# A two-block transformer on one core: the mixing stage of block 2 in a new order

## The chip, the cores and the metric

The kernel runs on 1 core of one Trainium2 chip. The metric is device time in microseconds, the median over several executions. The engines are TensorE (PE, with its weight loads as PEld), VectorE (DVE), ScalarE (ACT) and GpSimd (POOL); SyncE (SP) and ScalarE's queue issue transfers.

## The reference

A sequence of 512 positions of width 1024 passes through two blocks in float32. Block 1 mixes three branches (a short convolution, block-sparse attention with relative bias, attention to a memory), merges them through gates, multiplies by `w_out` and runs a convolutional feed-forward layer (`w_up`, `w_down`). Block 2, whose mixing is what changes:

```python
h = rmsnorm_2(x, norm_mix)
hq, hf, hi, hg, sq, sk, sv, iq, ik, iw, mq = split_in(h @ w_in)
o_hg = hgrn2_mix(hq, hf, hi, hg, ...)       # 4 heads, gated recurrence, rmsnorm per head, times silu(hg)
o_sa = dsa_mix(sq, sk, sv, iq, ik, iw, ...) # 8 index heads score keys; 128 kept per query; 4 attention heads
o_mem = mem_mix(mq, rmsnorm_2(mem, norm_mem), w_mem_kv, ...)  # 4 heads over 256 memory rows
x = x + concat(o_hg, o_sa, o_mem) @ w_out
a, b = split(rmsnorm_2(x, norm_ffn) @ w_ffn_in)
x = x + (silu(a) * b) @ w_ffn_out
```

## The kernel before

Every matrix product of weights is done in three passes with a high and a low part of both operands (lines 175 to 177): hi*hi, hi*lo, lo*hi. A weight tile is 128 x 1024 floats (512 KB). `load` (line 185) brings it into one of 3 raw buffers by SP's queue; `split` (line 190) makes its high part by a cast on ScalarE (line 197) and its low part by a subtraction (line 198), on VectorE or, while `on_pool` is set, on GpSimd. One tile is 24 matmuls, mostly of 512 columns.

The order of all instructions is written out once by the class `Program`; each engine runs its own in that order. A job takes its weight tiles and issues its matmuls in parts; after each part, and after each job, `tick` lets every background generator advance by its rate: 0.5 is one step at every second tick. `start` begins a generator, `drain` steps all of them until the named one has ended, `ctl` places a function between jobs. Before each job, `run` issues the splits of tiles up to two ahead (six for the resident tiles of an output product's second half), and the raw loads up to three beyond.

- `head_chunks` runs the first chunks of a stage in two halves of 256 positions, so that the first half can start while the last positions are still normalized and transposed (`late`). `chunk` gives features on partitions, `gemm_N` gives positions on partitions. `gemm_out` is an output product of two 512-column halves; `need` names the generators that are drained before a tile of its first half.
- HGRN (`hgrn_levels`): for each of 4 heads, 10 levels. A level is subtracted on GpSimd (lines 1254 to 1261), exponentiated on ScalarE (1266 to 1271), scaled on VectorE (1274) and multiplied on TensorE (1283 to 1308), each a step later than the one before; the small levels are merged by a masked copy (1314). `gates(j)` prepares the pair of heads j from `w_hf` and `w_hq`. `hgrn_tail` makes the outputs per 128 positions for all four heads, with norm and gate, and transposes them.
- The index (`idx`): scores of 8 heads (lines 990 to 995), then 16 rounds of maximum and replacement for each of three query blocks (`top_keys`, lines 1007 and 1008), on VectorE.
- Attention (`sa_pair`, `causal_pair`): scores, softmax (592, 601), transposes, product (618). Memory attention (`mem2_pair`, `mem_heads`) is alike; its keys and values come from `memT2.build` (norm and transposes of mem_2) and `w_mkv2`.

The order in `mixing` before: head with `w_hf` and `w_hq` of the first pair; `w_ikw`; four `w_iq`; four `w_mqsv`; drain of `memT2`; four half tiles of `w_mkv2`; four `w_sqk`; `w_hf` and `w_hq` of the second pair; four `w_hi`; four `w_hg`; drain of `hgrn`; then `w_out_2`, which needs `mem2`, `sa0` and `sa1`, and `tail`, in this order.

## Time and profile before

| | |
|---|---|
| median of 3 runs | 1565.33 us (1564.37 to 1567.9) |
| the profiled execution | 1568.02 us, its span 1566.2 us |
| mean granted clock of TensorE | 0.986 of full speed |
| TensorE busy | 1520.0 us (97%) |
| VectorE, ScalarE, GpSimd busy | 789.3, 597.5, 238.3 us |

A matmul's busy time is modelled and overlaps the next one's. The granted clock has two levels, 1.00 (2.4 GHz) and 0.50 (1.2 GHz); a figure between them is a mean over a stretch. Busy time of VectorE counts overlapping instructions once in a table by stage, and each in full in a table by line.

### The profile page before, as it was taken

Reading aid. Unit: us, or ns where it says so; the run is one execution under the profiler, and the core shown is the slowest. Engines: PE = TensorE matmul, PEld = TensorE weight load, DVE = VectorE, ACT = ScalarE, POOL = GpSimd, SP = SyncE. Lnnn points to the kernel's source line nnn. Section 1 sums busy time; section 2 is a strip of 40 time slices with the busy share of each in tenths; the row PEclk is TensorE's granted clock in tenths of the full one; section 3 lists DMA queues with packets and bytes.
Section 4 is the critical chain, followed back from the end, with each engine's and each line's share of the span. In section 5 each row is a group of like instructions: output and inputs, shape, how many; then the busy total and the mean of one; then the engine's idle time right before and its main releaser. Section 6 shows DMA issues by size and latency. Waiting matters only on the chain.

```text
span 1566.2 us, 20399 instructions
## 1 busy us (share of the span) xinstructions
PE 1520.0 (97%) x8107; PEld 1261.1 (81%) x8107; DVE 789.3 (50%) x1200; ACT 597.5 (38%) x1043; POOL 238.3 (15%) x344
## 2 busy tenths in 40 slices
PE   8999999999999999999999999999789999999999
PEld 7887888888888888888888977677568888888887
DVE  5455453544446666665235488988545233333231
ACT  5454452433343433333234465455533222222120
POOL 1000000021102000000002197716220000000000
PEclk9999999999999999999999999999699999999999
DMA  5432243322252122223232331122222122222231
GB/s 187 99 106 73 83 128 108 121 81 81 96 164 78 68 95 99 102 96 107 95 137 92 115 119 70 68 75 82 68 81 81 68 94 95 94 102 100 94 121 54
DMA packets 46053, 151.83 MB, mean 97 GB/s; under 512 B 5476, under 2 KB 5988, under 8 KB 45958
## 3 DMA queue, kind: packets, MB, share of 16 engines
q1 hardware_dynamic: 41472, 142.62, 26.6%
q10 hardware_dynamic: 4486, 7.90, 1.8%
q8 instruction: 64, 1.05, 0.3%
q14 instruction: 31, 0.25, 0.0%
HBM read 145.66 MB, written 4.85 MB: 96 GB/s over the span
## 4 chain that ended last, share of the span: by engine, by line
PE 82%; DVE 7%; ACT 4%; POOL 2%; issue 2%; DMA 2%; ACTq 0%; SPq 0%; DVEq 0%; POOLq 0%
PE p L175 26%; PE p L176 26%; PE p L177 26%; PE p L307 2%; ACT s L592 1%; DVE s L1008 1%; DVE s L1274 1%; DVE m L1007 1%; PE p L618 1%; ACT s L601 1%; POOL m L228 1%; DVE wl L198 1%; DMA s<-mem 0%; POOL s L183 0%; DVE s L180 0%
## 5 line engine op out<-in xcount | busy, mean ns | idle before, releaser
L175 PE MATMUL p<-s,wh 128*128 128x512 f32 (+1 forms) x1192 | 463.6, 389 | 0.9 <-DVE t L1314 0.6
L176 PE MATMUL p<-s,wh 128*128 128x512 f32 (+1 forms) x1192 | 461.0, 387 | 0.0
L177 PE MATMUL p<-s,wl 128*128 128x512 f32 (+1 forms) x1192 | 460.7, 387 | 0.0
L198 DVE TENSOR_TENSOR wl<-r,wh 128x1024 fp32r<-128x1024 f32 x217 | 258.3, 1192 | 329.8 <-ACT wh L197 329.0
L197 ACT CAST wh<-r 128x1024 fp32r<-128x1024 f32 x233 | 232.9, 1002 | 230.8 <-PE p L176 219.2
L175 PEld LDWEIGHTS p<-s,wh 128*128 128x128 f32 x1192 | 224.0, 188 | 46.3 <-DVE t L1314 0.8
L177 PEld LDWEIGHTS p<-s,wl 128*128 128x128 f32 x1192 | 223.9, 188 | 45.5
L176 PEld LDWEIGHTS p<-s,wh 128*128 128x128 f32 x1192 | 224.0, 188 | 43.9
L175 PE MATMUL p<-wh,s 128*128 128x512 f32 x544 | 218.6, 402 | 4.1 <-ACT s L270 4.1
L177 PE MATMUL p<-wh,s 128*128 128x512 f32 x544 | 215.2, 396 | 1.0 <-DVE s L275 0.5
L176 PE MATMUL p<-wl,s 128*128 128x512 f32 x544 | 214.8, 395 | 0.0
L176 PE MATMUL p<-s,s 128*128 128x256 f32 (+1 forms) x408 | 132.2, 324 | 5.6 <-DVE s L180 5.6
L175 PE MATMUL p<-s,s 128*128 128x256 f32 (+1 forms) x408 | 133.2, 326 | 0.9 <-ACT s L268 0.8
L177 PE MATMUL p<-s,s 128*128 128x256 f32 (+1 forms) x408 | 131.6, 322 | 0.0
L183 POOL TENSOR_SCALAR s<-t 128x512 fp32r<-128x512 f32 (+1 forms) x64 | 34.7, 543 | 618.3 <-DVE t L1506 227.4
L175 PEld LDWEIGHTS p<-wh,s 128*128 128x128 f32 x544 | 104.0, 191 | 26.3 <-ACT s L270 4.5
L177 PEld LDWEIGHTS p<-wh,s 128*128 128x128 f32 x544 | 103.8, 191 | 24.2 <-DVE s L275 1.0
L176 PEld LDWEIGHTS p<-wl,s 128*128 128x128 f32 x544 | 104.1, 191 | 20.5
L176 PEld LDWEIGHTS p<-s,s 128*128 128x128 f32 x408 | 79.5, 195 | 11.9 <-DVE s L180 6.6
L175 PEld LDWEIGHTS p<-s,s 128*128 128x128 f32 x408 | 79.4, 195 | 7.1 <-ACT s L268 1.5
L177 PEld LDWEIGHTS p<-s,s 128*128 128x128 f32 x408 | 79.5, 195 | 5.3
L307 PE MATMUL p<-ident,s 128*128 128x128 f32 x400 | 59.7, 290 | 16.2 <-ACT s L601 4.8
(182 smaller groups left out, 1416.1 us busy)
## 6 DMA issues: line engine op xcount, KB each, us to landing
r<-w_up SPq DMA_DIRECT2D x44, 512.0 KB, 3.2
r<-w_ffn_in SPq DMA_DIRECT2D x44, 512.0 KB, 3.2
r<-w_in_gate SPq DMA_DIRECT2D x24, 512.0 KB, 3.2
r<-w_down SPq DMA_DIRECT2D x22, 512.0 KB, 3.2
r<-w_ffn_out SPq DMA_DIRECT2D x22, 512.0 KB, 3.2
r<-w_out SPq DMA_DIRECT2D x16, 512.0 KB, 3.2
r<-w_in_conv SPq DMA_DIRECT2D x12, 512.0 KB, 3.2
r<-w_in_qk SPq DMA_DIRECT2D x8, 512.0 KB, 4.6
```

Source lines behind the costliest of these rows:

```text
L175: mm(out, sh, mh, start=start, stop=False)
L176: mm(out, sh, ml, start=False, stop=False)
L177: mm(out, sl, mh, start=False, stop=stop)
L183: g_.tensor_scalar(out, x, s, 0.0, op0=ALU.mult, op1=ALU.add)
L197: a_.copy(hi[:, :n], raw)
L198: (g_ if on_pool else v_).tensor_tensor(out=lo[:, :n], in0=raw, in1=hi[:, :n].bitcast(F32), op=ALU.subtract)
L228: g_.tensor_tensor(out=rs, in0=ms, in1=negh[:, :n], op=ALU.pow)
L307: pe.transpose(ps[:m, n:n + P], s, ident)
L592: a_.activation(pv, pv, AF.Exp, scale=-1.0, bias=negm[s][:, i:i + 1], accum_out=sums[s][:, i:i + 1])
L601: a_.activation(pv, pv, AF.Copy, scale=rec[s][:, i:i + 1])
L618: mm(ps[64 * s:64 * s + 64, j * P:512], vh(s, j), p_view(PT, s, 3 - j), start=(j == 0), stop=(j == 3))
L1007: v_.max(m8, sc)
```

## The change

`split` always subtracts on VectorE; `on_pool` is gone. `memT2` is built during the last gate of block 1, and `w_mkv2` multiplied at the first boundary, between `w_out` and the up-projection's head, which then has two chunks instead of four. The finished keys and values go to DRAM and come back in the mixing by six transfers on SP. The mixing begins with the index's weights; `hgrn` steps at 0.7 and `idx` at 0.85 instead of 0.5 and 0.6; the second pair of gates comes earlier; the two attention pairs are one chain at 0.5; the HGRN tail is done per pair of heads and 256 positions, with the gate applied after the transposes; `w_hg` is last and is laid out with features on partitions.

```diff
-        (g_ if on_pool else v_).tensor_tensor(out=lo[:, :n], in0=raw, in1=hi[:, :n].bitcast(F32), op=ALU.subtract)
+        v_.tensor_tensor(out=lo[:, :n], in0=raw, in1=hi[:, :n].bitcast(F32), op=ALU.subtract)
...
     for m in range(KD):
+        if m == 3:
+            pr.start("memT2", lambda: memT2.build())
         gate(2, m, use_bc(m, True))
+    pr.drain("memT2")
...
+    def filled_head(late, srcs, uses):
+
+        def first():
+            late[0](2)
+            late[1]()
+        head_chunks(srcs, H, uses, {(0, 0): first, (0, 1): lambda: late[0](3)})
...
-    next_head((late, swap), [W[0], W[NFF], W[1], W[NFF + 1]], [use_up_a(0), use_up_g(0), use_up_a(1), use_up_g(1)])
-    for j in range(2, NFF):
+    gemm_N([io["w_mkv2"][i] for i in range(4)], lambda: memT2, lambda t, ps: use_mkv2(t, ps), nt=2)
+    filled_head((late, swap), [W[0], W[NFF]], [use_up_a(0), use_up_g(0)])
+    pr.start("kv2", lambda: fin_mkv2())
+    for j in range(1, NFF):
...
-        yield
+        yield from wait(2)
+        st["kvd"] = drp.tile([3, P, 1024], F32, name="kvd")
+        for n, x in enumerate((m2.pop("kh").all, m2.pop("kl").all, m2.pop("v"))):
+            nc.sync.dma_start(st["kvd"][n], x.rearrange("p a b -> p (a b)").bitcast(F32))
+
+    def load_kv2():
+        m2["kh"], m2["kl"], m2["v"] = Heads(256), Heads(256), slot([P, 4, 256])
+        for n, x in enumerate((m2["kh"].all, m2["kl"].all, m2["v"])):
+            nc.sync.dma_start(x.rearrange("p a b -> p (a b)").bitcast(F32), st["kvd"][n])
...
-    def use_hg(t, ps):
-        if t % 2 == 0:
-            gS[t // 2] = slot([P, 2, 512])
-        silu2(gS[t // 2][:, t % 2, :], ps)
+    def use_hg(c):
+        def f(ps):
+            if c % 2 == 0:
+                gS[c // 2] = slot([P, 2, 512])
+            silu2(gS[c // 2][:, c % 2, :], ps)
+            if c % 2:
+                hg["gate", c // 2] = True
+        return f
...
-        g_.tensor_tensor(out=y, in0=y, in1=gS[t // 2][:, t % 2, :], op=ALU.mult)
         return y
...
+    def hgrn_outT(j, tp, y):
+
+        pt = transposes([y[:, (2 * t + k) * P:(2 * t + k + 1) * P] for k in range(2) for t in range(2)])
+        cols = slice(tp * 256, tp * 256 + 256)
+        z = tmp()
+        v_.scalar_tensor_tensor(z.rearrange("p (k t) -> p k t", k=2), pt.rearrange("p (k t) -> p k t", k=2),
+                                vcol(V_HG), gS[j][:, :, cols], op0=ALU.mult, op1=ALU.mult)
+        mixed.alloc(j)
+        hi, lo = mixed.h[j][:, :, cols], mixed.l[j][:, :, cols]
+        z = z.rearrange("p (k t) -> p k t", k=2)
+        a_.copy(hi, z)
+        sub_lo(lo, z, hi)
+
+    def hgrn_tail(j):
+        def g():
+            while ("done", 2 * j + 1) not in hg:
+                yield
+            y1 = hgrn_out(j, 1)
+            yield from wait(2)
+            y0 = hgrn_out(j, 0)
+            yield from wait(2)
+            while ("gate", j) not in hg:
+                yield
+            hgrn_outT(j, 1, y1)
+            yield from wait(2)
+            hgrn_outT(j, 0, y0)
+        return g
...
     def mixing():
+        next_head((late2, swap2), M["w_ikw"] + M["w_iq"][:3], [use_ikw, use_iq(0), use_iq(1), use_iq(2)], park)
+        pr.start("idx", chain(sel0, index_weights, *(index_scores(c) for c in range(4)), top_keys(3),
+                              top_keys(2), top_keys(1)), 0.85)
+        pr.start("hgrn", hgrn_levels, 0.7)
+        chunk(M["w_iq"][3], H, use_iq(3))
+        for c in (0, 1):
+            chunk(M["w_hf"][c], H, use_hf(c))
+        for c in (0, 1):
+            chunk(M["w_hq"][c], H, use_hq(c))
         pr.start("gates0", gates(0))
+        gemm_N(M["w_mqsv"], H, use_mqsv)
+        pr.ctl(load_kv2)
+        pr.start("finm", fin_mq)
+        for c in (2, 3):
+            chunk(M["w_hf"][c], H, use_hf(c))
+        pr.drain("finm")
+        pr.start("mem2", chain(mem2_pair(0), mem2_pair(1)), 0.5)
+        for c in (2, 3):
+            chunk(M["w_hq"][c], H, use_hq(c))
+        pr.start("gates1", gates(1))
+        gemm_N(M["w_sqk"], H, use_sqk)
+        pr.start("fin", fin_sqk)
+        gemm_N(M["w_hi"], H, use_hi)
+        pr.start("tail0", hgrn_tail(0))
+        pr.start("sa", chain(sa_pair(0), sa_pair(1)), 0.5)
+        pr.start("tail1", hgrn_tail(1))
         for c in range(4):
+            chunk(M["w_hg"][c], H, use_hg(c))
...
-             need={0: ("mem2",), 1: ("sa0", "sa1"), 2: ("tail",)})
+             need={0: ("mem2",), 1: ("sa",), 2: ("tail0", "tail1")})
...
-    io["w_hg"] = _pack_n(w[:, 1536:2048])
+    io["w_hg"] = _pack_t(w[:, 1536:2048])
```

The lines of the old `mixing` that go are left out here; its order is told above.

## Rows read from the trace of the kernel before

**Rows 1.** The page: the span, the busy time of each engine with its share and number of instructions, and the granted clock in 40 equal slices, in tenths.
```profile
span 1566.2 us, 20399 instructions
...
PE 1520.0 (97%) x8107; PEld 1261.1 (81%) x8107; DVE 789.3 (50%) x1200; ACT 597.5 (38%) x1043; POOL 238.3 (15%) x344
...
PEclk9999999999999999999999999999699999999999
```

**Rows 2.** The table by stage: stretch in us, its length, then busy time and number of instructions for PE, PEld, DVE, ACT and POOL, the mean granted clock, the DMA engines' share and GB/s.
```profile
477.00:503.00 26.00, 22.99 (x150) 21.05 (x149) 17.99 (x34) 11.62 (x34) 6.29 (x13) 0.93 0.19 61
...
912.00:944.00 32.00, 26.07 (x176) 20.67 (x175) 26.63 (x29) 19.59 (x44) 25.67 (x26) 1.00 0.35 126
944.00:969.00 25.00, 25.00 (x260) 19.61 (x259) 19.64 (x39) 16.88 (x35) 19.22 (x19) 0.93 0.22 77
969.00:998.00 29.00, 28.18 (x269) 21.91 (x267) 26.48 (x52) 13.45 (x26) 23.57 (x27) 1.00 0.29 99
998.00:1034.00 36.00, 33.59 (x226) 25.40 (x227) 33.12 (x77) 17.98 (x43) 16.48 (x21) 1.00 0.16 56
1034.00:1069.00 35.00, 31.85 (x136) 23.43 (x134) 27.04 (x56) 19.62 (x39) 13.90 (x30) 0.95 0.17 57
1069.00:1098.00 29.00, 29.00 (x315) 22.83 (x317) 24.44 (x60) 16.45 (x35) 13.55 (x18) 1.00 0.26 92
1098.00:1126.00 28.00, 16.55 (x295) 14.09 (x286) 18.89 (x70) 18.09 (x49) 10.23 (x20) 0.55 0.24 77
1126.00:1150.00 24.00, 23.27 (x161) 18.80 (x160) 9.36 (x16) 6.52 (x12) 9.24 (x14) 0.95 0.07 23
1150.00:1162.00 12.00, 7.42 (x39) 5.57 (x37) 8.46 (x11) 7.54 (x12) 1.48 (x2) 1.00 0.48 168
1162.00:1171.00 9.00, 8.48 (x24) 6.37 (x25) 1.64 (x5) 0.27 (x1) 0.00 (x0) 0.62 0.35 126
```

**Rows 3.** The same table for a quiet stretch of block 2's feed-forward layer.
```profile
1240.00:1280.00 40.00, 40.00 (x178) 33.14 (x177) 12.83 (x14) 9.90 (x12) 1.86 (x3) 1.00 0.31 105
```

**Rows 4.** The chain that ended last, 921 to 945 us: start, length, what.
```profile
922.23 7.52 DMA s<-mem
```

**Rows 5.** The same chain, 1148 to 1165 us.
```profile
1154.12 3.22 DMA r<-w_out
...
1157.42 1.05 ACT s L197
```

**Rows 6.** The list of transfers: what, queue, how many, size of each, median us from issue to landing.
```profile
s<-xdram SPq DMA_DIRECT2D x4, 512.0 KB, 4.0
```

**Rows 7.** VectorE's instructions by line, 882 to 1165 us: out<-in, shapes, number, total busy us, mean ns of one, idle time before them.
```profile
L1274 DVE TENSOR_TENSOR s<-s,s 128x256 f32<-128x256 f32 x36 | 28.8, 800 | 2.7 <-ACT s L1271 2.7
L1007 DVE MAX8 m<-s 128x8 f32<-128x512 f32 (+2 forms) x48 | 26.5, 552 | 0.2
L1008 DVE MATCH_REPLACE8 s<-m,s 128x512 f32<-128x512 f32 (+2 forms) x48 | 26.0, 542 | 0.0
...
L1056 DVE SCALAR_TENSOR_TENSOR s<-p,gsc,s 64x256 fp32r<-64x256 f32 x16 | 7.7, 483 | 2.4 <-ACT s L1054 2.1
...
L1314 DVE COPY_PREDICATED t<-lmask,p 128x128 f32<-128x128 uint32 x24 | 7.1, 295 | 2.6 <-PE p L1308 1.4 <-POOL t L1312 1.2
L993 DVE TENSOR_SCALAR s<-t,iw 128x512 f32<-128x512 f32 (+2 forms) x3 | 5.6, 1855 | 1.5 <-ACT t L990 1.4
...
L633 DVE TENSOR_REDUCE m<-p 128x2 f32<-128x512 f32 x8 | 5.5, 682 | 0.0
L1065 DVE SCALAR_TENSOR_TENSOR s<-p,vecs,s 128x256 fp32r<-128x256 f32 x12 | 5.2, 477 | 0.1
...
L1033 DVE TENSOR_REDUCE m<-t 128x4 f32<-128x256 f32 (+1 forms) x10 | 5.1, 522 | 4.1 <-ACT t L1031 4.1
L1183 DVE TENSOR_TENSOR_SCAN s<-t,t 128x512 f32<-128x512 f32 x4 | 4.9, 1225 | 0.1
L198 DVE TENSOR_TENSOR s<-r,s 128x1024 fp32r<-128x1024 f32 x4 | 4.8, 1220 | 3.3 <-ACT s L197 3.3
...
L1008 DVE MATCH_VALUE_LOAD s<-m,s 128x8 f32 x48 | 4.4, 92 | 1.7
```

**Rows 8.** Line 1274 over the whole span: duration in ns, shortest, median and longest; first and last start.
```profile
L1274 DVE TENSOR_TENSOR s<-s,s x36: 411/474/2607, 917.3 to 1113.4; 128x256 f32<-128x256 f32 x36
```

**Rows 9.** TensorE in order of time, 1087 to 1088 us: start, length, line, operation, number.
```profile
1087.26 0.46 PE L1308 MATMUL p<-s 128*32 128x32 f32 x32
1087.65 0.50 PE L175 MATMUL p<-wh,s 128*128 128x512 f32 x1
```

**Rows 10.** GpSimd's instructions by line, 882 to 1165 us, columns as in rows 7.
```profile
L198 POOL TENSOR_TENSOR wl<-r,wh 128x1024 fp32r<-128x1024 f32 x16 | 39.1, 2445 | 14.6 <-ACT wh L197 11.3 <-issue 3.0 <-DVE s L1274 0.3
```

**Rows 11.** VectorE in order of time, from 923 to 930 us and from 1059 to 1061 us, columns as in rows 9.
```profile
925.01 2.61 DVE L1274 TENSOR_TENSOR s<-s,s 128x256 f32<-128x256 f32 x1
...
1059.37 1.98 DVE L198 TENSOR_TENSOR wl<-r,wh 128x1024 fp32r<-128x1024 f32 x1 [0.94 <-ACT wh L197]
```

**Rows 12.** GpSimd in order of time, from 923 to 929 us.
```profile
924.63 2.70 POOL L198 TENSOR_TENSOR wl<-r,wh 128x1024 fp32r<-128x1024 f32 x1
```

**Rows 13.** ScalarE in order of time, from 1113 to 1127 us; a row can merge many instructions of a line.
```profile
1118.16 7.33 ACT L601 ACTIVATE s<-s,m 128x512 f32<-128x512 f32 x16
```

92 lines of the change are left out of this document (28 added, 64 removed).

## The prediction, made before the changed kernel was run

> **What bounds the kernel now.** I read the page first: TensorE (PE) is busy 97% of the span [rows 1], so time can only come from stretches where it waits or runs at the lower of its two clock levels. The table by stage finds them [rows 2]. A quiet stage issues 178 matmuls of 512 columns in 40 us, 0.225 us each [rows 3]; any stage with PE under its own length, or PEclk under 1.00, loses against that. Read idle time as length minus PE, and the clock's share as (1 - PEclk) times PE's busy time (times the length where PE is nearly always busy).
>
> - 477 to 503, from `w_out` to the up-projection's head: 3.0 idle and 1.8 of clock, 4.8 us.
> - 912 to 969, the drain of `memT2`: 5.9 idle and 1.8 of clock, 7.7 us. The longest piece of its chain is the load of mem_2, 7.5 us [rows 4].
> - 969 to 1098: 0.8 + 2.4 + 3.2 idle and 1.8 of clock, 8.2 us. Here VectorE (DVE) is the neighbour at its limit: 33.1 of 36 us in one stage.
> - 1098 to 1126, the drain of `hgrn`: 11.5 idle, and 0.45 of the 16.5 busy, 7.4: 18.9 us.
> - 1126 to 1150: 0.7 idle and 1.2 of clock; 1150 to 1171: 4.6 + 0.5 idle and 3.2 of clock. Together 10.2 us. The chain shows weight loads and ScalarE's casts of them ahead of the last HGRN output on that engine [rows 5].
>
> The sum is 49.8 us. The second boundary, from `w_down` to the mixing's head, is left as it is and counts in neither sum.
>
> **What the change does, in beats.** A weight tile is 24 matmuls in four ticks ("beats") of six. A background generator advances by its rate at each beat, so the order of instructions follows from counting. From the mixing head's end I count, after the change: index scores to beat 23.5 (20 steps at 0.85); the 51 top-key steps from there to 84; `gates0` from 20, its pair ready at 30; HGRN heads 0 and 1 to 58, heads 2 and 3 from 62 (`gates1` starts at 52) to 90, the pipe empty at 96; `mem2` from 44 to 78; `w_hi` done at 84; gate done at 100; `w_out_2`'s first tile to 104. Before, `gates1` came after beat 76, and 20 levels at 0.5 need 40 beats, while the gate ends at 108: that is why its drain is expensive. In the new order no level is left to drain, and the HGRN tails lie beside the gate's 16 beats.
>
> **First boundary.** `mkv2` is four half tiles, 48 x 0.225 = 10.8 us of PE between `w_out`'s last tile and the head's transposes. It covers the wait there: -4.8. These 10.8 us, the sixteen `memT2` transposes and eight K transposes leave the mixing, so PE's own work is unchanged in total. `memT2`'s loads have some 30 beats in the last gate chunks: the 7.7 us go. The three stores and three loads of K and V are 512 KB each on SP, where the reloads of x landed in 4.0 us [rows 6]. What is queued behind them are raw weight tiles, fetched about three tiles of 5.4 us before their split; 12 us of transfers fit, so I cost them at nothing, up to 4 us without that cover. The two-chunk head in halves is within 1 us.
>
> **The middle, beats 23.5 to 84.** Here I expect the cost. DVE work emitted there, by durations [rows 7]: top keys 26.5 + 26.0 + 4.4, 56.9; HGRN scaling, 33 of 36 at 0.53 (between the median 0.474 [rows 8] and the mean 0.800), 17.5; masked copies, 21 of 24 of 7.1, 6.2; splits, 15 x 1.22 = 18.3; both gates, scans 4.9 and four passes at 0.68 and two at 1.2, 10.0; memory attention, 5.5 and about 6.3 for its smaller pieces at the same rates, 11.8; head norms, 7.7 + 8/12 of 5.2 + 8/10 of 5.1 + 6 for twelve scalings at 0.41 to 0.68, 21.2; two SiLU at 0.68 and the masks, 2.5. Sum 144 us.
>
> PE in the same beats: 60.5 x 6 x 0.225 = 81.7 for weights. For the rest I take 969 to 1098: 129 us less the 8.2 lost, less 16 tiles of 5.4, leaves 34.4; with 15 more HGRN products at 0.6 (0.39 until the next tile's matmul, which itself is 0.1 late, and 0.1 ahead of it [rows 9]), and about 2 us less of attention scores: 41. So 123 us. DVE exceeds PE by 21 us. PE can run ahead by about one HGRN step, for its products need the scaling emitted a step earlier: 2 us of cover. The middle loses 19 us where its counterpart lost 8.2.
>
> The split belongs in this sum twice. On GpSimd it took 2.4 us a tile [rows 10], on DVE it takes 1.2. But while GpSimd worked on one, from 924.6 to 927.3, a DVE multiply of that line took 2.61 [rows 11, 12], where its shortest took 0.41; over 36 multiplies the mean stands 0.33 above the median, 11.7 us, and three index multiplications averaged 1.86 [rows 7]. Freed of that, DVE gets back about what the splits cost. The Trainium skill's SBUF — State Buffer, section "Who interferes with whom", says that a DVE instruction with two SBUF inputs contends with a GpSimd instruction that reads SBUF, and that one waits for the whole of the other; the trace agrees (2.61 beside 0.41). Another rule speaks against the change: Perfetto Trace Analysis, section "Optimizing Scalar/DVE Operations", holds that some work of a saturated DVE may be worth handing to GpSimd, with a warning on the shared port. If the long multiplies were only costly by their layout, the sum would keep 0.80 for each, +9 us, and give 1557, the end of the forecast's own range; by the lock it gives the forecast below.
>
> **The end.** Attention is now one chain at 0.5 from beat 84. It makes 10 of 17 steps before `w_out_2` needs it at 104, so the drain exposes the second pair's last scores, softmax, transposes and product. On the bounds: scaling 16 blocks took ScalarE 7.3 us for two pairs [rows 13], so 3.7 for one; with four exponentials at the same 0.46 (1.8), the first subtraction (0.5), score matmuls (0.8), two rounds of transposes and copies (2.2) and the product (2.2) the chain is 11.2 us, of which PE works some 5. Idle: 7 us, between 4 (other generators left to fill) and the 18.9 that the old drain cost. `put` hides behind the six matmuls of the first pair. The tails' outputs are through before `w_out_2` prepares its resident tiles, so casts that wait for loads no longer stand ahead of them: the 10.2 us go.
>
> For a clock dip at the drain 1.8 (as after `memT2`'s), the tails' own waits 1.9 (what 1126 to 1150 lost), and a remnant at the first boundary of 2: 5.7 us.
>
> **Sum.** Gained 49.8; lost again 19 + 7 + 5.7 = 31.7; net 18 us. The profiled execution took 1568.0 us, its span 1566.2; that gives 1550. The median of the runs is 1565.3, 2.7 below it, so the forecast for the median is 1548.
>
> **Rivals.**
> 1. DVE keeps pace: the splits stand two tiles ahead of use, and this slack absorbs most of the middle, which loses 4 us. For it: in 998 to 1034 DVE was busy 92% and PE lost only 2.4 us. Against it: the HGRN products have no such lead. 1548 - 15 = 1533. Chance 0.17.
> 2. The drain at `w_out_2` only changes its name and costs 18.9 like the old one. For it: the same softmax stood in the old drain. Against: that one also had ten HGRN levels. 1548 + 12 = 1560. Chance 0.17.
> 3. Slower: the splits are moved into a contention with GpSimd's HGRN subtractions. One DVE split beside such work took 1.98 us [rows 11], and multiplies up to 0.8. If all 15 take 1.98 (+11.3) and all scalings 0.80 (+9), the middle loses 39, the net is -2, and the median 1568; from an extra 21 us on it is slower by more than a measurement tells, and with an index multiplication or a late K/V load on top 1571. Against: GpSimd loses 12 of its splits in this stage (29 us), so such overlaps should get rarer. Chance 0.18.
>
> **Chances and range.** My forecast has 0.48, with a range of its own from 1540 to 1557: 7 us each way on DVE's sum and 4 to 14 for the drain. Differences below 0.2%, 3 us, can't be told from no change. Faster takes the forecast, rival 1 and most of rival 2's (what falls short of 1562): 0.70. Within 3 us: the rest of rival 2 and the near end of rival 3, 0.12. Slower: 0.18. The range reaches to rival 1's 1533 and to 1567, where rival 3 begins.
>
> **What the profile of the changed kernel would show.** No PE wait and full clock between `w_out` and the up-projection; no wait of a transpose on `memT2`'s subtraction; no GpSimd line L198, and L1274 near 0.5 us; from the index phase's end to `w_hi` DVE above 92% busy and PE losing about 19 us, with HGRN products waiting for L1274's line; one gap of 7 us or more at attention's last softmax, a clock dip behind it, and then `w_out_2` without a wait on loads. I am wrong if PE's idle time in the middle is under 8 or over 30 us, if the drain costs more than 16, or if SP's waits for a free slot make weights late.

## The result: slower by 13.6 us, and the profile after

The changed kernel took 1580.26 us, the median of four runs (1577.07 to 1583.3), against 1566.62 us for the kernel before beside it: a ratio of 1.0087, 95% interval 1.0061 to 1.0114. The forecast of 1548 us missed by 32 us, and the sign was wrong. The profiled execution took 1577.07 us, its span 1575.3.

Lines move in the changed kernel: HGRN's scale multiply, line 1274 before, is 1298; its products, 1283 to 1308, are 1307 to 1332; the product of its output is 1431.

The page of the changed kernel, the lines that answer to [rows 1]:

```profile
span 1575.3 us, 20298 instructions
...
PE 1516.7 (96%) x8059; PEld 1256.0 (80%) x8059; DVE 789.9 (50%) x1216; ACT 597.0 (38%) x1039; POOL 188.1 (12%) x325
...
PEclk9999999999999999999999998989899999999999
```

TensorE's busy time is 3 us below that of before and the span 9 us longer, so the added time is waiting and half clock. GpSimd lost 50 us of work, VectorE gained none.

The table by stage of the changed kernel, columns as in [rows 2]: the first boundary, the last gates and the mixing's head, two pieces of the middle and the middle as a whole, the prediction's middle from the last index score to `w_hi` (942 to 1096 us), the second head pair's tail, what lies between, and the wait of the output projection on the attention.

```profile
480.00:512.00 32.00, 29.23 (x154) 24.80 (x154) 21.20 (x36) 14.49 (x34) 6.73 (x15) 0.89 0.30 97
897.00:927.00 30.00, 30.00 (x141) 25.03 (x140) 17.82 (x26) 14.83 (x27) 0.00 (x0) 1.00 0.22 75
927.00:953.00 26.00, 26.00 (x121) 21.71 (x120) 18.80 (x32) 14.99 (x21) 1.09 (x1) 1.00 0.19 67
...
953.00:966.00 13.00, 3.07 (x11) 2.21 (x10) 12.24 (x25) 5.00 (x13) 10.24 (x25) 0.72 0.36 124
...
1020.00:1040.00 20.00, 13.34 (x173) 8.26 (x171) 16.26 (x34) 3.56 (x7) 6.54 (x15) 0.83 0.15 53
...
953.00:1080.00 127.00, 97.12 (x934) 72.44 (x933) 109.40 (x246) 66.37 (x141) 72.46 (x130) 0.91 0.19 65
...
942.00:1096.00 154.00, 124.12 (x1146) 92.85 (x1145) 131.63 (x295) 76.52 (x158) 79.93 (x142) 0.92 0.18 64
...
1122.00:1134.00 12.00, 4.25 (x54) 3.78 (x53) 2.99 (x5) 5.17 (x10) 1.17 (x4) 0.67 0.13 44
1134.00:1157.00 23.00, 23.00 (x129) 18.74 (x128) 12.98 (x22) 8.59 (x15) 2.79 (x6) 0.95 0.36 137
1157.00:1172.00 15.00, 10.98 (x57) 8.60 (x56) 6.22 (x20) 10.43 (x26) 0.00 (x0) 0.77 0.00 1
```

Read with the prediction's measure, idle time plus (1 - PEclk) times PE's busy time, the losses stand in three places. First boundary: 2.8 + 3.2 = 6.0 us, where the prediction left a remnant of 2. Middle, 953 to 1080: 29.9 + 8.7 = 38.6 us, where it put 19. End: 7.75 + 1.4 ahead of the second tail, 1.15 between, 4.0 + 2.5 at the attention, 16.8 us, where it put 7 + 3.7 (the clock's 1.8 and the tails' 1.9). The two new waits are 10 us at the first HGRN product and 7.7 us at the second pair's output.

TensorE's waits in the changed kernel, over the whole span: line, for whom, us in total, times, longest.

```profile
PE p L1307 <- DVE s L1298: 9.9, 1, 9.9
PE p L1332 <- DVE s L1298: 9.5, 5, 6.1
PE p L1431 <- POOL s L183: 7.7, 1, 7.7
PE p L307 <- ACT s L601: 5.2, 2, 4.0
```

The chain that ended last shows why the first product came so late: start, length, what.

```profile
941.92 0.70 DVE t L1206
...
943.78 1.20 DVE wl L198
...
949.60 1.14 DVE s L1209
950.76 1.07 ACT s L1211
...
951.91 3.50 POOL s L1213 x2
...
957.87 0.61 POOL s L1278
...
959.62 1.04 ACT wh L197
960.69 1.22 DVE wl L198
...
963.63 0.34 DVE s L1298
...
964.11 2.05 PE p L1307 x4
```

This is the first pair's gate: from VectorE to ScalarE (1211), to GpSimd (two additions, 3.5 us, then the small offsets until 957.9, then the first level's additions), to the exponential on ScalarE (line 1295), and past a weight cast and a weight split that stand in the same queues, to the scale and the product. The chain takes 22.2 us from the first of these rows to the product: some 14 are its own steps with the handovers between them, and 8 are other work ahead of them in the queues of VectorE (top keys, splits, small reductions) and ScalarE (the cast). TensorE reached the product at 954 and every tile behind it waited too, for 9.9 us.

What the prediction had right is also in the rows. The scale multiply, to be held against [rows 8] (shortest, median, longest):

```profile
L1298 DVE TENSOR_TENSOR s<-s,s x36: 411/418/1285, 963.5 to 1117.1; 128x256 f32<-128x256 f32 x36
```

Its longest fell from 2.607 to 1.285 us and its median from 0.474 to 0.418. And the transfers of the keys and values, to be held against [rows 6]:

```profile
kvd<-s SPq DMA_DIRECT2D x3, 512.0 KB, 4.4
s<-kvd SPq DMA_DIRECT2D x3, 512.0 KB, 4.1
```

TensorE's only wait on a transfer in the whole span is 2.2 us on a gain of block 1, so these six cost nothing visible.

### The profile page after: what moved, and what is told of

Same layout as the page of the kernel before. It is cut to its first block, busy times and chain, and to the rows that moved or that the text cites. A ratio compares the mean times of both kernels' runs of the same rounds, so it can differ in the third digit from the quotient of the medians.

```text
span 1575.3 us, 20298 instructions
## 1 busy us (share of the span) xinstructions
PE 1516.7 (96%) x8059; PEld 1256.0 (80%) x8059; DVE 789.9 (50%) x1216; ACT 597.0 (38%) x1039; POOL 188.1 (12%) x325
## 4 chain that ended last, share of the span: by engine, by line
PE 84%; DVE 5%; ACT 4%; issue 3%; POOL 3%; DMA 0%; ACTq 0%; SPq 0%; DVEq 0%; POOLq 0%
PE p L175 26%; PE p L176 26%; PE p L177 26%; PE p L307 2%; DVE wl L198 1%; PE p L618 1%; ACT s L592 1%; DVE s L1023 1%; PE p L1431 1%; DVE m L1022 1%; POOL s L183 1%; POOL m L228 0%; ACT s L601 0%; PE p L559 0%; POOL s L1213 0%
## 5 line engine op out<-in xcount | busy, mean ns | idle before, releaser
L175 PE MATMUL p<-s,wh 128*128 128x512 f32 (+1 forms) x1240 | 485.3, 391 | 0.0
L176 PE MATMUL p<-s,wh 128*128 128x512 f32 (+1 forms) x1240 | 480.3, 387 | 0.0
L177 PE MATMUL p<-s,wl 128*128 128x512 f32 (+1 forms) x1240 | 480.1, 387 | 0.0
L198 DVE TENSOR_TENSOR wl<-r,wh 128x1024 fp32r<-128x1024 f32 x235 | 279.4, 1191 | 331.1 <-ACT wh L197 330.2
L175 PEld LDWEIGHTS p<-s,wh 128*128 128x128 f32 x1240 | 233.6, 188 | 46.4 <-issue 0.7
L176 PEld LDWEIGHTS p<-s,wh 128*128 128x128 f32 x1240 | 233.6, 188 | 44.9
L175 PE MATMUL p<-wh,s 128*128 128x512 f32 x512 | 204.3, 399 | 3.7 <-ACT s L637 1.8
L176 PE MATMUL p<-wl,s 128*128 128x512 f32 x512 | 201.7, 394 | 2.2 <-DVE wl L198 2.2
L177 PE MATMUL p<-wh,s 128*128 128x512 f32 x512 | 201.2, 393 | 0.0
L176 PE MATMUL p<-s,s 128*128 128x256 f32 (+1 forms) x376 | 122.0, 325 | 2.9 <-DVE s L180 2.9
L175 PE MATMUL p<-s,s 128*128 128x256 f32 (+1 forms) x376 | 123.2, 328 | 0.2 <-ACT s L268 0.2
L177 PE MATMUL p<-s,s 128*128 128x256 f32 (+1 forms) x376 | 121.6, 324 | 0.0
L175 PEld LDWEIGHTS p<-wh,s 128*128 128x128 f32 x512 | 97.4, 190 | 25.6 <-ACT s L637 2.2
L177 PEld LDWEIGHTS p<-wh,s 128*128 128x128 f32 x512 | 97.4, 190 | 20.8
L176 PEld LDWEIGHTS p<-s,s 128*128 128x128 f32 x376 | 72.4, 193 | 9.1 <-DVE s L180 3.7
L175 PEld LDWEIGHTS p<-s,s 128*128 128x128 f32 x376 | 72.4, 193 | 6.4 <-ACT s L268 0.9
L177 PEld LDWEIGHTS p<-s,s 128*128 128x128 f32 x376 | 72.4, 192 | 5.3
L931 ACT ACTIVATE t<-p,vecs 128x512 f32<-128x512 f32 x44 | 34.3, 781 | 110.5 <-PE p L177 110.5
```

The source lines that it names most:

```text
L175: mm(out, sh, mh, start=start, stop=False)
L176: mm(out, sh, ml, start=False, stop=False)
L177: mm(out, sl, mh, start=False, stop=stop)
L198: v_.tensor_tensor(out=lo[:, :n], in0=raw, in1=hi[:, :n].bitcast(F32), op=ALU.subtract)
L931: a_.activation(u, ps, AF.Identity, scale=vcol(V_FCW + 2 * 2 * NFF + c), bias=vcol(V_FCB + c))
```

## The experiments

Each ratio is to the kernel before, measured beside it; 0.001 is 1.6 us. Each interval is 3 to 8 us wide, so a difference of two ratios is known to 2 to 4 us. Two theories stood at first: the middle is set by the amount of VectorE's work (the prediction's), or by the latency of chains that cross the queues.

Where ratios are close, a second measure helps. Ahead of the mixing, e5, e2, e3 and e6 are the same program, yet the last Gelu of block 1 (line 939) starts between 743.8 and 750.3 us in their profiles. So the stretch from there to the first SiLU of block 2 (line 1539) is compared too. It holds all of the mixing and is called the mixing's stretch below; in the changed kernel it takes 482.0 us (744.8 to 1226.8), in e5 482.1, in e4, which differs only ahead of it, 483.6. It comes from one execution of each kernel and is known to 1 or 2 us.

### e5: the changed kernel again

> The changed kernel as it is, beside the next three on one chip, so that they can be compared with it: 1580 in the first comparison, ratio 1.0087. Both theories expect a ratio within 0.3% of that.

1.0086 (1.0070 to 1.0102). This is what the edits of the changed kernel are compared with.

### e1: the splits alone

```diff
-        pr.on_pool = True
+        pr.on_pool = False
```

> The kernel before with one part of the change alone: the 16 weight splits that GpSimd did in the mixing are done on VectorE. Theory of the port (a VectorE operation with two SBUF inputs waits while GpSimd works on a split): VectorE takes over 16 x 1.22 = 19.5 us and gets back about 17 us of stretched multiplies, so the median stays within 5 us of the kernel before and the mean of the HGRN multiplies (line 1274) falls from 0.80 to about 0.53 us. Rival, that the offloading paid: line 1274 keeps a mean near 0.8 and the kernel is 10 us or more slower than before.

0.9983 (0.9974 to 0.9992): 2.7 us faster than before. In the kernel before so edited, the multiply of [rows 8] reads:

```profile
L1274 DVE TENSOR_TENSOR s<-s,s x36: 411/420/957, 915.2 to 1112.0; 128x256 f32<-128x256 f32 x36
```

Its longest fell from 2.607 to 0.957 us although VectorE took on 16 splits. This part of the change is good; the loss comes from elsewhere.

### e2: half of the top-key rounds

```diff
-            for r in range(16):
+            for r in range(8):
```

> The changed kernel with 8 instead of 16 rounds of maximum and replacement per query block, so 64 instead of 128 keys are taken out and the selection is not the reference's. It takes 24 rounds, 24 x (0.55 + 0.54 + 0.09) = 28 us, of VectorE's work out of the middle. If VectorE's amount of work sets the pace there (the theory of the prediction), TensorE's loss between the first HGRN product and the end of w_hi shrinks by some 20 us and the kernel is 15 to 20 us faster than the changed one (about 1562). Rival, that fixed latencies of the HGRN chain set it (gates, GpSimd, ScalarE, scaling, in 5 to 6 beats): the 10 us wait of the first product stays above 7 us, and the kernel gains less than 8 us (1572 or more).

1.0029 (1.0018 to 1.0039), 9 us under the changed kernel. The edit leaves out half of the selection, some 28 us of VectorE's work. A third of it came back as time by the ratio, and less by the mixing's stretch, 477.0 us against 482.0; 953 to 1080 us still loses 32 us (PE busy for 101.9 at a mean clock of 0.93) against 38.6. VectorE's amount is a part of the loss, not most of it. The 9.9 us ahead of the first product stayed, but say less: eight rounds of top keys stand in that stretch in both kernels.

### e3: HGRN's heads made ready later

```diff
             hgrn_offsets(j)
-            yield from wait(2)
+            yield from wait(8)
```

> The changed kernel with the HGRN levels of each pair released 6 steps later (wait of 8 instead of 2 at the end of the gates' generator), nothing else. If the 10 us wait of the first product (and the 6 us one at the second pair) is only an order in which TensorE comes before its data, the first wait falls from 9.9 to under 3 us and the middle gains 8 to 12 us; the levels end 6 beats later, which can cost up to that much at the drain of the tails. Whole: 1570 to 1580. Rival, that VectorE's queue is behind by a fixed amount of work: the waits only move to later products and the middle's loss stays within 3 us.

1.0055 (1.0040 to 1.0070), 5 us under the changed kernel; but the mixing's stretch is 483.9 us against 482.0, so the edit gained nothing where it acts. The wait shrank from 9.9 to 3.9 us, but 4.5 us appeared ahead of transposes that wait for VectorE's line 1055, and 4.6 us ahead of others that wait for ScalarE's 656. PE was busy for 100.6 us of 953 to 1080 at a mean clock of 0.89, a loss of 37.5 against 38.6. The wait had moved.

### e4: the memory's weights split ahead of the first boundary

```diff
-    gemm_N([io["w_mkv2"][i] for i in range(4)], lambda: memT2, lambda t, ps: use_mkv2(t, ps), nt=2)
+    gemm_N([io["w_mkv2"][i] for i in range(4)], lambda: memT2, lambda t, ps: use_mkv2(t, ps), nt=2, kind="hold")
```

> The changed kernel with the four w_mkv2 tiles prepared up to four tiles ahead into resident slots, instead of two ahead. In the changed kernel the casts of the third and fourth tile stand behind the last block's norm on ScalarE and VectorE, and TensorE waits 3.2 us for them and loses 1.5 to 2.5 more to the clock. If that order is the cause, the boundary's loss falls from 7.9 to under 3 us and the kernel is about 5 us faster than the changed one (1575). Rival, that the norm chain itself is late: the wait moves to the head's transposes and nothing is gained.

(`gemm_N` hands `kind` on to its jobs.) 1.0044 (1.0029 to 1.0059), 6.6 us under the changed kernel. From 480 to 512 us PE is now busy throughout at full clock:

```profile
480.00:512.00 32.00, 32.00 (x202) 28.79 (x201) 21.06 (x38) 15.61 (x41) 8.13 (x17) 1.00 0.25 79
```

The `w` tiles of `w_mkv2` are only two deep and 12 matmuls (2.7 us) each, and their casts and splits stood behind the last block's norm; in the changed kernel TensorE waited 0.6 and 2.2 us for them and its mean clock fell to 0.89. (The clock's share is not in every execution: e3 and e6 have the same two waits and show 1.00 in this stretch.) Held four ahead, they do what the prediction assumed.

### e7: the memory's move alone, in the old order

The kernel before with every split on VectorE, `memT2` built beside the last gate, `w_mkv2` at the first boundary (held ahead as in e4), and the reload behind `w_mqsv` (store, reload and the shorter head are those of the change and not shown again):

```diff
     for m in range(KD):
+        if m == 3:
+            pr.start("memT2", lambda: memT2.build())
         gate(2, m, use_bc(m, True))
+    pr.drain("memT2")
...
+    gemm_N([io["w_mkv2"][i] for i in range(4)], lambda: memT2, lambda t, ps: use_mkv2(t, ps), nt=2, kind="hold")
...
-        pr.start("memT2", memT2.build)
         gemm_N([io["w_mqsv"][j] for j in range(4)], H, use_mqsv)
+        pr.ctl(load_kv2)
         pr.start("finm", fin_mq)
-        pr.drain("memT2")
-        gemm_N([io["w_mkv2"][j] for j in range(4)], lambda: memT2, use_mkv2, nt=2)
-        pr.start("mem2", chain(fin_mkv2, mem2_pair(0), mem2_pair(1)), 0.5)
+        pr.start("mem2", chain(lambda: wait(5), mem2_pair(0), mem2_pair(1)), 0.5)
```

> The old order of the mixing with the other two parts of the change: splits on VectorE, memT2 in the last gate and w_mkv2 at the first boundary (its tiles prepared four ahead, as in e4), K and V reloaded after w_mqsv. If what is lost lies in the new order of the mixing and not in these parts, this kernel is faster than the one before: splits -3 (e1), the drain of memT2 -5 to -8, the first boundary -3; whole 1553 to 1560, ratio 0.991 to 0.995. Rival, that the memory work was a useful filler in the mixing: TensorE loses there what the boundary gains, and the ratio stays between 0.997 and 1.003.

1.0032 (1.0020 to 1.0044), 7.7 us **over** e1, though 12.5 us of the prediction's gains belong to this move. So the memory's tiles may have been worth something where they stood, which the next run tests.

### e13: the move, with useless matmuls at the old place

```diff
         pr.start("finm", fin_mq)
+        gemm_N([io["w_mqsv"][j] for j in range(4)], H, lambda t, ps: a_.copy(small(1), ps[:, 0:1]), nt=2)
         pr.start("mem2", chain(lambda: wait(5), mem2_pair(0), mem2_pair(1)), 0.5)
```

> e7 (old order, the memory's tiles moved to the first boundary) with 48 useless matmuls of 512 columns (10.8 us, four weight tiles with their loads and splits) put at the memory's old place in the mixing; their result goes nowhere. Theory (the moved tiles had been cover for the chains): TensorE does 10.8 us more and the time grows by at most 4 us over e7, ratio 1.002 to 1.006; the waits at 980 to 1020 us and at 1130 to 1155 us shrink by 7 us or more together. Rival (the move costs by the reload, by the slots it holds or by its work at the new place): the 10.8 us come on top of e7, ratio 1.009 to 1.012.

1.0019 (1.0009 to 1.0028): with 10.8 us more for TensorE the kernel is no slower than e7; the 2 us by which it is faster lie within the two intervals. The table by stage shows where (columns as in [rows 2]); first e1, nothing moved:

```profile
480.00:550.00 70.00, 67.35 (x393) 59.90 (x392) 43.15 (x65) 27.13 (x47) 7.34 (x14) 0.98 0.18 61
850.00:980.00 130.00, 125.63 (x950) 106.24 (x948) 93.88 (x154) 77.09 (x149) 56.37 (x84) 0.99 0.29 100
980.00:1020.00 40.00, 34.47 (x281) 27.01 (x280) 35.05 (x78) 18.52 (x46) 11.00 (x18) 0.91 0.17 55
...
1120.00:1180.00 60.00, 53.37 (x292) 42.81 (x291) 27.60 (x40) 24.88 (x46) 10.73 (x16) 0.92 0.22 72
```

e7, moved:

```profile
480.00:550.00 70.00, 68.89 (x370) 59.24 (x369) 45.62 (x70) 32.81 (x64) 10.01 (x20) 1.00 0.31 104
850.00:980.00 130.00, 127.69 (x884) 108.58 (x883) 86.66 (x145) 71.10 (x141) 51.79 (x80) 0.99 0.27 92
980.00:1020.00 40.00, 30.20 (x265) 22.55 (x264) 30.26 (x65) 20.84 (x49) 13.23 (x20) 0.83 0.12 40
...
1120.00:1180.00 60.00, 47.02 (x270) 39.74 (x270) 26.16 (x57) 26.07 (x60) 10.76 (x16) 0.86 0.19 62
```

e13, moved and filled again:

```profile
480.00:550.00 70.00, 68.90 (x365) 59.07 (x365) 45.44 (x69) 32.05 (x62) 10.16 (x21) 1.00 0.29 99
850.00:980.00 130.00, 128.05 (x896) 108.71 (x895) 88.89 (x145) 73.75 (x145) 54.60 (x84) 0.99 0.29 100
980.00:1020.00 40.00, 34.19 (x340) 26.45 (x340) 34.89 (x76) 17.58 (x42) 12.42 (x21) 0.96 0.17 55
...
1120.00:1180.00 60.00, 50.95 (x316) 41.11 (x307) 24.45 (x42) 25.88 (x55) 11.87 (x20) 0.87 0.18 63
```

By idle plus clock, e1 loses 4.0, 5.6, 8.6 and 10.9 us in these four stretches. The move takes 2.9 out of the first and 2.0 out of the second, as it was meant to, and puts 6.3 into the third (14.9) and 8.7 into the fourth (19.6). With the useless tiles they fall to 7.2 and 15.7. The two stretches left out differ by under 1 us between e1 and e7, and behind 1180 us e1 loses another 1.3. The measure is rough, for the fixed limits catch slightly different work in each run: all in all it makes the move 8 us dearer, the spans 7.6.

The mixing's stretch doesn't hang on such limits. Its two ends in e1, with the last exponential of the attention (line 592) and the rounds of top keys that start before `w_hi`'s first product is copied (number behind the x):

```profile
L926 ACT ACTIVATE t<-t x22: 632/632/634, 509.2 to 728.7; 128x512 f32<-128x512 f32 x22
...
L1500 ACT ACTIVATE t<-p x22: 598/599/600, 1214.1 to 1433.7; 128x512 f32<-128x512 f32 x22
...
L592 ACT ACTIVATE s<-s,m x48: 384/554/724, 68.7 to 1116.4; 128x512 f32<-128x512 f32 x12, 128x384 f32<-128x384 f32 x12, 128x256 f32<-128x256 f32 x12, 128x128 f32<-128x128 f32 x12
...
L1007 DVE MAX8 m<-s x29: 547/680/695, 956.2 to 1062.8; 128x8 f32<-128x512 f32 x16, 128x8 f32<-128x384 f32 x13
```

The same in e7:

```profile
L936 ACT ACTIVATE t<-t x22: 630/632/633, 513.6 to 740.4; 128x512 f32<-128x512 f32 x22
...
L1517 ACT ACTIVATE t<-p x22: 598/599/600, 1221.6 to 1441.2; 128x512 f32<-128x512 f32 x22
...
L592 ACT ACTIVATE s<-s,m x48: 386/555/727, 69.5 to 1138.3; 128x512 f32<-128x512 f32 x12, 128x384 f32<-128x384 f32 x12, 128x256 f32<-128x256 f32 x12, 128x128 f32<-128x128 f32 x12
...
L1019 DVE MAX8 m<-s x24: 547/683/695, 963.6 to 1064.3; 128x8 f32<-128x512 f32 x16, 128x8 f32<-128x384 f32 x8
```

And in e13:

```profile
L936 ACT ACTIVATE t<-t x22: 631/632/633, 512.6 to 739.4; 128x512 f32<-128x512 f32 x22
...
L1518 ACT ACTIVATE t<-p x22: 598/598/599, 1219.6 to 1439.2; 128x512 f32<-128x512 f32 x22
...
L592 ACT ACTIVATE s<-s,m x48: 384/555/725, 68.4 to 1120.5; 128x512 f32<-128x512 f32 x12, 128x384 f32<-128x384 f32 x12, 128x256 f32<-128x256 f32 x12, 128x128 f32<-128x128 f32 x12
...
L1019 DVE MAX8 m<-s x29: 547/682/694, 962.7 to 1069.2; 128x8 f32<-128x512 f32 x16, 128x8 f32<-128x384 f32 x13
```

The stretch takes 485.4, 481.2 and 480.2 us. The move took 10.8 us of matmuls and the memory's transposes out of it and shortened it by 4.2; with the useless tiles in, it is no longer than without. The memory's tiles, then, had been work that TensorE did while chains on the other engines ran: moving them emptied the place, and useless work fills it as well.

A tile brings matmuls and also beats that advance the chains; the run puts both back and doesn't tell them apart. But the beats have left a mark. Four half tiles are eight beats, in which the index, at 0.6, takes about five steps: 24 rounds of top keys have started in e7 where e1 and e13 have 29. The attention waits for their result, and from the last Gelu to its last exponential it takes 387.7 us in e1, 397.9 in e7 and 381.1 in e13. No run raised the index's rate in place of the tiles.

### e15: the transposes moved alone

```diff
     for m in range(KD):
+        if m == 3:
+            pr.start("memT2", lambda: memT2.build())
         gate(2, m, use_bc(m, True))
+    pr.drain("memT2")
...
-        pr.start("memT2", memT2.build)
...
-        pr.drain("memT2")
```

> e1 with the memory's transposes built beside the third gate of block 1, as the change has them, and the keys and values kept in the mixing: no reload from DRAM, and no wait for the transposes. The first half of the forecast's memory term (7.7 us of the drain at 912 to 944 us, of which e1 still shows 3.4 us above clean matmuls). Theory of the forecast: 3 us or more under e1, ratio 0.996 or less. Rival (what is taken out of the mixing comes back later as the chains' waits): within 2 us of e1 or over it, ratio 0.997 to 1.001.

0.9983 (0.9974 to 0.9992), just e1's. Here the drain's wait goes (850 to 980 us: PE busy for 127.6 of 130 against 125.6), and the same 2 us come back elsewhere. What e1 had left of the prediction's drain of 7.7 us was worth nothing in the end.

### e9 and e12: which part of the new order costs

e9 is e1 with the HGRN tail by head pair, the gate last, and the attention as one chain behind `w_hi`, where e1 starts its two pairs side by side ahead of it:

```diff
-        pr.start("sa0", sa_pair(0), 0.5)
-        pr.start("sa1", sa_pair(1), 0.5)
...
         gemm_N(M["w_hi"], H, use_hi)
-        gemm_N([io["w_hg"][j] for j in range(4)], H, use_hg)
-        pr.drain("hgrn")
-        pr.start("tail", hgrn_tail, 1.0)
+        pr.start("tail0", hgrn_tail(0))
+        pr.start("sa", chain(sa_pair(0), sa_pair(1)), 0.5)
+        pr.start("tail1", hgrn_tail(1))
+        for c in range(4):
+            chunk(M["w_hg"][c], H, use_hg(c))
```

> The kernel before with three of the change's parts: every split on VectorE, the HGRN tail by head pair, and the gate's tiles last; the mixing's tiles stay in the order of before and the memory's keys and values stay in the mixing. Both attention pairs run in one chain, as in the change. Theory (the cost of the change comes from the index queries in front and from the memory's tiles taken out of the mixing, the tail itself gains): the drain of 1098 to 1126 (18.9 us in the table by stage) falls to about half, since the first pair's tail, the gate's tiles and the first parts of the output projection lie beside HGRN's last products: ratio 0.990 to 0.995 (8 to 15 us under the kernel before). Rival (the tail by head pair only moves the drain behind the gate's tiles, as the 7.9 us ahead of the second pair's tail in the changed kernel suggest): ratio 0.997 to 1.003.

0.9982 (0.9970 to 0.9993), e1's again. The old drain is shorter (1100 to 1120: PE busy for 12.4 us at 0.83, against 10.4 at 0.64 in e1) and 1120 to 1180 worse (50.2 us at 0.83, against 53.4 at 0.92), with one wait of 4.9 us on the attention's line 601. The loss moved, as the rival had it. But it is the attention that is waited for now, and e9 also starts the attention later; no run has the new tail with the old attention, so what the tail would give by itself isn't known.

e12 is the changed kernel with e4's edit and the tiles in the order of before, rates 0.5 and 0.6 too, and against e9 it differs by the memory's move alone:

```diff
-        next_head((late2, swap2), M["w_ikw"] + M["w_iq"][:3], [use_ikw, use_iq(0), use_iq(1), use_iq(2)], park)
+        next_head((late2, swap2), M["w_hf"][:2] + M["w_hq"][:2], [use_hf(0), use_hf(1), use_hq(0), use_hq(1)], park)
+        pr.start("gates0", gates(0))
+        pr.start("hgrn", hgrn_levels, 0.5)
...
-        pr.drain("finm")
-        pr.start("mem2", chain(mem2_pair(0), mem2_pair(1)), 0.5)
+        pr.start("mem2", chain(lambda: wait(5), mem2_pair(0), mem2_pair(1)), 0.5)
```

> The changed kernel, memory weights held ahead at the boundary (as e4), with the mixing's tiles in the order of before (first head pair, index key and queries, memory queries, self-attention, second head pair, HGRN input, gate); tail by head pair and gate last stay. Undoes the index queries first alone. Theory (queries first put HGRN's first product 10 us ahead of its data, and that part is what costs most in the middle): no wait above 3 us at HGRN's first product, a ratio of 0.996 to 1.001, 5 to 13 us under e4. Rival (the queries' place is harmless and the waits come from the memory's tiles that are missing in the mixing, as in e7): ratio 1.002 to 1.006, with the waits at the end of the mixing as in e7.

1.0052 (1.0035 to 1.0068): 11 us over e9, so the move costs here too (24 rounds of top keys have started before `w_hi`'s first copy, 29 in e9); and 1 us over e4, so the queries in front, with the rates and the earlier second pair that go with them, cost nothing that can be told, although they are what makes the 9.9 us wait. Without it the same time is lost at other places.

### e11: useless matmuls in the new order

```diff
         pr.start("gates0", gates(0))
+        gemm_N(M["w_mqsv"], H, lambda t, ps: a_.copy(small(1), ps[:, 0:1]), nt=2)
```

> The changed kernel with its memory weights held ahead at the first boundary (as e4) and 48 useless matmuls of 512 columns (48 x 0.226 = 10.8 us; the shape of the memory's keys and values, four weight tiles, with their loads and splits) put behind the start of the first head pair's gates, where TensorE waits 9.9 us for HGRN's first product. Their result goes nowhere. Theory (the mixing lacks independent TensorE work beside its chains, and the memory's tiles that the change took out had been such work): the wait of 9.9 us falls under 2 us, later waits shrink with the beats gained, and the time is within 4 us of e4 (ratio 1.002 to 1.007) although TensorE does 10.8 us more. Rival (the memory's tiles were no cover, the chains run by VectorE's amount): the 10.8 us come on top, ratio 1.010 to 1.014.

1.0086 (1.0071 to 1.0101), 6.6 us over e4: between the two theories. Only 4 of the 10.8 us were free, and the wait ahead of the first product went from 9.9 to 7.3 us. HGRN's first product comes a fixed number of beats after its gates, whichever tile gives the beats, so filler behind the gates' start doesn't push it back. That filler pays where it adds beats between a chain and what needs it, as in e13, is read from the order of the two programs and not tested by itself. For the changed order the runs show a cost of missing cover only to this extent.

### e6, e8, e10, e14, e16 to e18: repairs

e6: the changed kernel with one more step between product and scale.

```diff
-    HB = 5
-    LAG = ((), ("scale",), ("exp",), ("subtract",))
+    HB = 6
+    LAG = ((), ("scale",), (), ("exp",), ("subtract",))
```

> The changed kernel with one more empty step in the HGRN pipe, between the exponential and the scaling (six level buffers instead of five; one slot more, paid for with one temporary less). VectorE has the same work. If the waits of HGRN products in the middle come from latency (GpSimd, ScalarE and VectorE one after another in fewer steps than they need), the later products wait much less: the five waits of the small products, 9.5 us, fall under 4, the middle gains 5 to 10 us, the kernel lies near 1572. Rival, that VectorE's backlog is the cause: a step of 1.4 beats only moves the waits, the middle's loss stays within 3 us and the kernel within 4 us of the changed one.

1.0059 (1.0044 to 1.0074), 4 us under e5, but none of it in the mixing's stretch (481.8 us against 482.0). The waits of HGRN's products stay (L1307 10.3, L1332 9.5 us).

e8: e4, a wait of three beats ahead of each tail, and the attention at 0.85 instead of 0.5.

```diff
+            yield from wait(3)
             y1 = hgrn_out(j, 1)
...
-        pr.start("sa", chain(sa_pair(0), sa_pair(1)), 0.5)
+        pr.start("sa", chain(sa_pair(0), sa_pair(1)), 0.85)
```

> The changed kernel with three repairs of waits that its trace shows: the w_mkv2 tiles prepared four ahead (as in e4), each HGRN tail begun three steps after its last level, and attention at 0.85 steps per beat instead of 0.5, so that its 17 steps fit into the 20 beats before w_out_2 needs it. If each wait is an order in which TensorE comes before its data, the boundary gives 6, the tail's wait of 7.7 falls under 3 and attention's waits of 4.0 and the clock behind it fall by 3 to 5: whole 1562 to 1567, ratio 0.998 to 1.001. Rival, that these chains are already as short as their engines allow: tail and attention give under 4 us together, ratio 1.002 or more.

1.0037 (1.0023 to 1.0051), 1 us under e4. The wait of 7.7 us ahead of line 1431 is gone, and from 1087 to 1180 us these are TensorE's longest waits:

```profile
PE p L175 <- DVE s L1438: 4.2, 1, 4.2
PE p L307 <- ACT s L601: 2.4, 2, 1.4
PE p L307 <- DVE s L1438: 2.1, 1, 2.1
```

With two smaller ones they sum to 10.3 us, where e4 has 12.3 in this stretch (7.8, 4.0 and 0.5): most of the waiting was divided, not removed.

e10: e9 with the second pair's tiles and gates ahead of `w_sqk`.

```diff
-        gemm_N(M["w_sqk"], H, use_sqk)
-        pr.start("fin", fin_sqk)
...
         pr.start("gates1", gates(1))
+        gemm_N(M["w_sqk"], H, use_sqk)
+        pr.start("fin", fin_sqk)
```

> As e9_tail_alone, with the second head pair's tiles and gates one step earlier, ahead of the self-attention's queries and keys: HGRN's second pair starts 4 tiles (4 x 24 x 0.226 = 21.7 us) earlier and has more tiles beside it. Theory (what HGRN lacks at the end is cover by tiles): the wait ahead of the second pair's tail goes, and the ratio is 3 to 8 us under that of e9. Rival (the attention, now 4 tiles later, becomes what the output projection waits for): within 3 us of e9, or over it, with the wait on the exponentials of the attention.

1.0030 (1.0014 to 1.0045), 7.5 us over e9. HGRN's drain goes (1100 to 1120: PE busy for 17.3 us at full clock), and the attention's softmax takes its place: 1120 to 1180 holds 42.5 us at 0.77, and line 601 is waited for three times, 9.8 us.

e14: e1 with e6's `HB` and `LAG`.

> e1 (the kernel before, every split on VectorE) with one more buffer and one more step between HGRN's product and its scale (HB 6, as in e6). Theory (the drain at 1096 to 1118 us waits step by step for the scale on VectorE, 1 to 2.4 us each, 10 us in all): the drain's waits fall by a third to a half, ratio 0.994 to 0.997. Rival (VectorE's and ScalarE's throughput sets the drain, not the distance of the steps): ratio 0.998 to 1.000, and the waits move to a later step.

0.9993 (0.9978 to 1.0008): no gain over e1.

e16 and e18: e1 with HGRN's rate at 0.7, and at 0.45.

```diff
-        pr.start("hgrn", hgrn_levels, 0.5)
+        pr.start("hgrn", hgrn_levels, 0.7)
```

and 0.45 in place of 0.7.

> e1 with HGRN's rate 0.7 in place of 0.5 (the change's rate). Theory (the chain's own latency sets the drain): HGRN's steps come earlier, wait in the middle instead, and the second pair still starts with its gates: within 2 us of e1, ratio 0.997 to 1.000. Rival (HGRN is only paced too slowly): the drain at 1096 to 1118 us falls by half, ratio 0.992 to 0.996.

> e1 (the kernel before, every split on VectorE) with HGRN's rate 0.45 in place of 0.5. Theory (the rate of before lies near its best: slower, HGRN's drain at its end grows as fast as its waits in the middle fall): within 2 us of e1, ratio 0.997 to 0.9995. Rival (the rate's cost goes on falling, 10 us for the 0.2 from 0.7 to 0.5, so 2 to 3 us for 0.05): ratio 0.996 to 0.997.

0.7 gives 1.0051 (1.0032 to 1.0069), 0.45 gives 1.0036 (1.0023 to 1.0048): 11 and 8 us over e1. Too early, a product stops TensorE (8.0 us at its line 1283); too late, HGRN ends later: at 0.45 its last scale multiply starts at 1119.0 us against 1112.0 in e1, while `w_hi`'s first product is copied at the same time in both (1066.6 and 1066.7). Both theories of each run expected less.

e17: e4 with HGRN's rate back at 0.5.

```diff
-    rawp, wp, sp, tp, smp = pool("rawp", 3), pool("wp", 6), pool("sp", 38), pool("tp", 6), pool("smp", 24)
+    rawp, wp, sp, tp, smp = pool("rawp", 3), pool("wp", 6), pool("sp", 39), pool("tp", 5), pool("smp", 24)
...
-        pr.start("hgrn", hgrn_levels, 0.7)
+        pr.start("hgrn", hgrn_levels, 0.5)
```

> The changed kernel, memory weights held ahead (as e4), HGRN's rate 0.5 as before in place of 0.7 (one more of the large buffers and one fewer of the temporaries, so that the slower HGRN finds room). Theory (a product that comes before its data stops TensorE and every tile behind it, so the rate alone costs, as 0.7 cost the old order 10 us in e16): the waits at HGRN's first products (9.9 us at 954 us, 6.3 us at 1026 us in the changed kernel) fall under 8 us together, ratio 0.997 to 1.001. Rival (the slower rate pushes HGRN's last level and the tails out over the end of the tiles): the waits move to the second pair's tail, ratio 1.003 to 1.007.

1.0034 (1.0021 to 1.0047), 2 us under e4, which can't be told from nothing. The first product's longest wait is 7.6 us, and 6.8 us ahead of the transposes of line 307 on the second tail are new, as the rival had it.

No version beat e1, e9 and e15. Taken part by part, from the parts added one after another: splits -2.7 us (e1), tail and gate 0 (e9), memory's move +11 (e12), queries in front with their rates -1 (e4), its weights not split ahead +6.6 (e5). These are differences along one path from the kernel before to e5, so they add up to e5's own 13.5 us but for rounding and are no check on it; along another path the parts could come out otherwise.

## Why the prediction was wrong

**The step that failed** is in the part on the first boundary: "These 10.8 us, the sixteen `memT2` transposes and eight K transposes leave the mixing, so PE's own work is unchanged in total." The total is unchanged, but where the work lies has a price, and the prediction put none. It counted 4.8 + 7.7 us as gained by the move and no loss in the mixing for the tiles that left it. e7 shows about 5 us gained in those two places and 15 lost in two others, by the rough measure; e12 over e9 and e7 over e1 give the move's net cost as 11 and 7.7 us. e13 shows why in the order of before: the moved work had been cover, by its matmuls or by its eight beats. In the changed order this is shown in part only, for e11's tiles, at another place, took back 4 of 10.8 us. The list of what lay in the mixing was complete; it treated TensorE's tiles as load there, when they were what hid and paced the chains. A part of their price did stand in the sum of the middle, where TensorE's 123 us without them were set against VectorE's 144, but as an amount of work and not as time that the chains need.

**The middle, 19 us.** It measured 38.6. The mechanism was wrong too. The prediction set VectorE's sum against TensorE's and expected VectorE above 92% busy; it was busy for 109.4 of 127 us, 86%, the same share as before (111.1 of 129 by [rows 2]). The amount had been forecast well: in the changed kernel VectorE's lines from 942 to 1096 us add up to 145 us, where the sum has 144. But that sum counts instructions that overlap each in full; counted once they fill 131.6 of the 154 us, so VectorE's excess over TensorE's 123 was some 9 us and not 21, and VectorE was idle for 22. e2, with 28 us of VectorE's work gone, gave back 5 (the mixing's stretch) to 9 (the ratio). The chain through 1206, 1211, 1213 and 1298 took 22 us, 14 of them its own steps. The prediction counted beats from start to "ready" and never put the durations of the chain's steps, queues included, against those beats.

**The remnant of 2 us at the first boundary** was 6.0 us, 6.6 in time (e4). The mechanism, cover by 10.8 us of matmuls, was right and e4 realises it; the prediction hadn't asked when those tiles' own casts and splits would come.

**The end.** The drain, put at 7 us and 1.8 of clock, was 4.0 and 2.5: 6.5 us for 8.8. The tails' 1.9 us were 9.2 with the clock; the masked copy and the four GpSimd scalings ahead of the first output weren't in the sum. But a better size would not have saved the forecast, as e8 shows: without this wait the time stays within 1 us of e4.

**The gain of 18.9 us from HGRN's drain** was taken as the whole drain. e9 has the tails and the gate beside it and is level with e1. "In the new order no level is left to drain" was true (1080 to 1122 us loses 0.5 us), but waits of the same kind stood at the attention and the tails instead; that it is the drain's own latency that went there is argued, not shown.

**What held.** The splits: long multiplies are the price of GpSimd's splits and go with them. The Trainium skill's SBUF — State Buffer, section "Who interferes with whom", says that a VectorE instruction with two SBUF inputs contends with a GpSimd instruction that reads SBUF; e1 agrees, 2.607 us down to 0.957 for the longest, and the whole program 2.7 us faster. The rule weighed against it is in the Trainium skill's Perfetto Trace Analysis, section "Optimizing Scalar/DVE Operations": some of a saturated VectorE's work may be worth handing to GpSimd, though between these two it might not help. Here it didn't: e1, which takes the work back, is 2.7 us faster. The transfers of keys and values cost nothing, and the drain of `memT2` has no wait left (897 to 953 us, PE fully busy).

**The rivals.** The third had the sign and 1568 to 1571 us, by a contention that did not occur: the multiplies are at 0.418 us. The case that happened, work taken out as cover, stood in none of them. Of the signs that would make the forecast wrong, idle time in the middle over 30 us came nearest (29.9, and 38.6 with the clock); the drain cost less than 16 us, and TensorE waited for no weight's transfer. (The forecast's own sum, 1565.3 less 18.1, leaves 1547 where the text says 1548.)

**Open.** What in the chains' timing makes HGRN's rate so sharp wasn't separated, nor was a tile's share as matmuls from its share as beats, nor the new tail from the later attention. No run puts the memory's own tiles back into the changed order with the queries in front.
